# A shared opening for two output pairs, and a rearranged end of the convolution mixer, in a two-layer encoder

## The chip, the cores and the metric

The kernel runs on one core of a Trainium2 chip. The metric is device time in microseconds (us) of one execution, as the median of several runs. Line numbers (L12) are those of the kernel before the change.

## The reference, cut to what matters

An encoder of two layers over 256 positions and 2048 channels. Each layer is a mixer and a feed-forward part with a residual sum after each; the mixer of layer 0 is a convolution module, that of layer 1 a differential attention.

```
h = rmsnorm(x, mix_norm[0])
u = h @ w_in + b_in                       # 2048 -> 4096, halves a and gate
u = a * sigmoid(gate)
u = causal_dwconv(u, dw_w, dw_b)          # 31 taps per channel
u = silu(layernorm(u)) @ w_out + b_out    # layernorm over the 2048 channels
x = x + u
x = x + conv_ffn(rmsnorm(x))              # 2048 -> 2 * 5632 -> 2048
x = x + diff_attention(rmsnorm(x))        # 16 heads, relative bias, causal by chunks of 64
x = x + conv_ffn(rmsnorm(x)); out = rmsnorm(x)
```

## The kernel before, in words

Channels lie on the 128 partitions and positions along the rows; the 2048 channels are 16 tiles (`KT`), and x is held as eight double tiles `X[pr]`. A weight is loaded as 512 KB tiles of 128 x 1024 fp32 (`raw`, L140, on SP's DMA queue, five buffers). Each is split into a rounded part `hi` (a cast on ACT, L150) and a remainder `lo` (a subtraction, L152, on DVE or, where the step says "g", on POOL). Activations are split in the same way (L279 on ACT, L280 on DVE). A product is three: hi by hi, hi by the activation's remainder, lo by hi (L229).

The program is a list of steps, one weight tile each (`step`, L197); `pair` (L215) makes four steps of one pair of output tiles, 96 products in all. `run` (L178) goes through the steps: `ahead` (L186) asks for the tile four steps on to be split, then come the step's products, then what was put off to this step (`at`, L166), then `every` and the step's `post`. A scheduler places the instructions on the engines in the order of a modelled time; `high_priority`, `manual_schedule` and `issue_after` steer it.

**The opening.** `setup` (L391) loads x and the first weight tiles in turn on SP's queue, splits x (16 tiles) and the first weights, sums the squares of x on DVE (L333) and calls `norm_cols` (L336: sums over channels on PE, L286, then the power -1/2 on POOL, L298) and `norm_rows` (L351: spreads the result over the partitions with products L292, ACT copies it to `rstd`). The products of `w_in` don't need `rstd`; `post` (L449) does. It scales a pair by `rstd` (L453), takes the sigmoid (L455) and writes `cpad` (L457). There are two PSUM buffers `pp`, so the third pair needs the first one's `post`. The lo tiles of pair 0 are made on DVE, those of pair 1 on DVE and POOL in turn, and of pairs 2 to 15 on POOL.

**The taps.** For the 31-tap convolution `post` writes `cpad` to DRAM (`ud`, L469) and reads it back as four shifted copies `R` (L473), both on ACT's queue. `diagonals` (L481, POOL) makes small diagonal matrices `dg` (L482), and for pair 0 also the 18 full ones of the last tile (L489). `taps` (L493) does 12 taps of a tile (20 of tile 13, 24 of tile 14) on PE five steps later (L498); DVE does the rest, six per step (`tap_step`, L529). The last tile (i = 15) has 18 taps on PE (L507) and 13 on DVE (L515 to L519).

**The end of the mixer.** `dev` (L562) subtracts a shift from each tile, squares it, and sums both: on POOL up to tile 13 (L582, L583), in `early` for tile 14 (L591, L592, sums over channels L286), in `late` for tile 15. `layernorm` (L601) makes mean and variance, the power on POOL (L616), rows by products (L292) and then normalizes (L629 to L633) and activates (L637 to L645) tile by tile; the products of `w_out` (L238, L239), the first two pairs of it in alternation, start with the first tile.

**Attention's tables.** `attn_setup` (L746) runs in front of the first feed-forward step. On POOL's queue it writes a 3 MB table of shifted biases to DRAM in one DMA (L759), and then 16 small ones put the mask into it (L766). `bias` (L848) loads one head's 128 KB from it on SP's queue.

## Time and profile before

| | |
|---|---|
| median of 3 runs | 2254.43 us (2253.42 to 2255.34) |
| the profiled execution, its own time | 2254.46 us |
| its span, first to last instruction | 2252.7 us |
| PE busy | 2205.2 us (98% of the span) |
| DVE, ACT, POOL busy | 1634.2, 1200.7, 273.5 us |
| mean granted TensorE clock | 0.991 |

PE is TensorE's products, DVE is VectorE, ACT is ScalarE, POOL is GpSimd, SP is the engine whose queue issues most DMAs. A row of a timeline gives the start and the duration, the engine, the line, what is written and read, and in brackets how long the engine stood idle before it and what released it. The clock column is the granted share of TensorE's clock, 1.00 at 2.4 GHz and 0.50 at 1.2 GHz.

### The profile page before, as it was taken

How to read it: one execution, taken by the hardware profiler on the slowest of the kernel's cores; microseconds unless marked ns; L12 is line 12 of the kernel's file. 1: busy time of each engine (PE TensorE's matmuls, PEld its weight loads, DVE VectorE, ACT ScalarE, POOL GpSimd, SP SyncE). 2: the span in 40 equal slices, each digit the busy share in tenths (PEclk: the TensorE clock that was granted, in tenths of full speed). 3: DMA queues.
4: the chain of work that ended last, by engine and by line, in shares of the span. 5: the costliest groups of instructions: out<-in, count | busy, mean ns of one | idle time of the engine just before them, and what ended most of it. 6: DMA issues, size and time to landing. Idle time of an engine off the chain costs nothing.

```text
span 2252.7 us, 34458 instructions
## 1 busy us (share of the span) xinstructions
PE 2205.2 (98%) x13238; PEld 1937.4 (86%) x13238; DVE 1634.2 (73%) x2471; ACT 1200.7 (53%) x1796; POOL 273.5 (12%) x181
## 2 busy tenths in 40 slices
PE   5999899999999999999999999999999999999998
PEld 5999788888888888888888888888888888888887
DVE  4788675877767777677777787767777677676774
ACT  4333454655545555455565665555555455554554
POOL 4788500100000000000100000100000000000002
PEclk8999999999999999999999999999999999999998
DMA  6677357866666666666655555566666666666662
GB/s 236 192 218 215 112 185 164 244 187 189 188 189 191 189 188 187 192 189 186 193 176 177 171 171 174 170 192 186 190 187 187 188 188 187 190 188 190 187 188 94
DMA packets 126004, 417.51 MB, mean 185 GB/s; under 512 B 14416, under 2 KB 26704, under 8 KB 125840
## 3 DMA queue, kind: packets, MB, share of 16 engines
q1 hardware_dynamic: 113040, 400.42, 57.2%
q10 hardware_dynamic: 11520, 11.45, 2.0%
q0 software_dynamic: 1280, 3.46, 1.3%
q8 instruction: 103, 1.69, 0.3%
q14 instruction: 61, 0.50, 0.1%
HBM read 407.55 MB, written 7.72 MB: 184 GB/s over the span
## 4 chain that ended last, share of the span: by engine, by line
PE 94%; DMA 2%; DVE 0%; issue 0%; ACT 0%; POOL 0%; ACTq 0%; POOLq 0%; DVEq 0%
PE pp L238 48%; PE pp L239 25%; PE pp L229 7%; PE pp L236 4%; PE pp L235 2%; PE pp L813 1%; PE pp L815 1%; PE pp L814 1%; DMA raw<-in_w_up_dram 1%; PE s L863 1%; PE s L498 1%; PE o L898 0%; DMA R<-ud 0%; PE t L498 0%; PE s L507 0%; DMA ud<-cpad 0%
## 5 line engine op out<-in xcount | busy, mean ns | idle before, releaser
L238 PE MATMUL pp<-act,hi 128*128 128x512 f32 x3902 | 1380.7, 396 | 5.8 <-DVE act L645 3.1
L239 PE MATMUL pp<-act,lo 128*128 128x256 f32 x3902 | 1095.7, 281 | 0.0
L150 ACT CAST hi<-raw 128x1024 fp32r<-128x1024 f32 x752 | 788.1, 1049 | 532.2 <-PE pp L238 186.2
L152 DVE TENSOR_TENSOR lo<-raw,hi 128x1024 fp32r<-128x1024 f32 x686 | 844.4, 1232 | 299.2 <-ACT hi L150 287.5
L238 PEld LDWEIGHTS pp<-act,hi 128*128 128x128 f32 x3902 | 732.5, 188 | 165.6 <-DVE act L645 3.4
L239 PEld LDWEIGHTS pp<-act,lo 128*128 128x128 f32 x3902 | 739.4, 189 | 10.2
L238 PE MATMUL pp<-actb,hi 128*128 128x512 f32 x856 | 308.5, 397 | 1.4 <-ACT hi L150 1.4
L239 PE MATMUL pp<-actb,lo 128*128 128x256 f32 x856 | 241.3, 282 | 0.8 <-DVE lo L152 0.8
L333 POOL TENSOR_TENSOR ssq<-ssq,Z 128x512 f32<-128x512 f32 x24 | 35.6, 1484 | 1518.4 <-ACT Z L329 1518.3
L229 PE MATMUL pp<-act,hi 128*128 128x256 f32 x1088 | 203.4, 289 | 9.0 <-ACT act L279 6.2
L238 PEld LDWEIGHTS pp<-actb,hi 128*128 128x128 f32 x856 | 161.3, 188 | 40.2 <-ACT hi L150 1.7
L229 PEld LDWEIGHTS pp<-act,hi 128*128 128x128 f32 x1088 | 173.7, 196 | 15.5 <-ACT act L279 6.2
L152 POOL TENSOR_TENSOR lo<-raw,hi 128x1024 fp32r<-128x1024 f32 x66 | 158.0, 2413 | 56.3 <-ACT hi L150 55.6
L239 PEld LDWEIGHTS pp<-actb,lo 128*128 128x128 f32 x856 | 162.6, 190 | 1.2 <-DVE lo L152 1.1
L266 ACT COPY E<-pp 128x512 f32<-128x512 f32 x104 | 60.9, 585 | 184.1 <-PE pp L236 184.1
L229 PE MATMUL pp<-act,lo 128*128 128x256 f32 x544 | 156.4, 288 | 2.0 <-POOL lo L152 1.5
L382 ACT COPY E<-pp 128x512 f32<-128x512 f32 x109 | 63.9, 586 | 170.7 <-PE pp L236 163.0
L268 DVE TENSOR_TENSOR E<-pp,E 128x512 f32<-128x512 f32 x104 | 71.9, 691 | 108.2 <-ACT E L266 108.2
L704 DVE SCALAR_TENSOR_TENSOR Y<-fpad,prm,Y 128x256 f32<-128x256 f32 x352 | 146.9, 478 | 0.0
L384 DVE TENSOR_TENSOR x<-pp,x 128x512 f32<-128x512 f32 x101 | 69.8, 691 | 87.8 <-ACT E L382 87.4
L701 ACT ACTIVATE Y<-fpad,prm 128x256 f32<-128x256 f32 x176 | 96.3, 595 | 48.3 <-DVE fpad L697 48.3
L229 PEld LDWEIGHTS pp<-act,lo 128*128 128x128 f32 x544 | 106.7, 196 | 2.4 <-POOL lo L152 1.7
(194 smaller groups left out, 1797.5 us busy)
## 6 DMA issues: line engine op xcount, KB each, us to landing
raw<-in_w_up_dram SPq DMA_DIRECT2D x352, 512.0 KB, 4.1
raw<-in_w_down_dram SPq DMA_DIRECT2D x176, 512.0 KB, 4.1
raw<-in_w_in_dram SPq DMA_DIRECT2D x64, 512.0 KB, 4.4
raw<-in_w_qk_dram SPq DMA_DIRECT2D x64, 512.0 KB, 3.6
raw<-in_w_out_dram SPq DMA_DIRECT2D x32, 512.0 KB, 3.8
raw<-in_w_v_dram SPq DMA_DIRECT2D x32, 512.0 KB, 3.7
raw<-in_w_o_dram SPq DMA_DIRECT2D x32, 512.0 KB, 3.8
R<-ud ACTq DMA_DIRECT2D x52, 132.0 KB, 4.8
```

The lines of the kernel that those rows point to most:

```text
L150: nc.scalar.copy(hi[:, :n], raw[:, :n])
L152: ins = eng.tensor_tensor(lo[:, :n], raw[:, :n], hi[:, :n].bitcast(F32), ALU.subtract)
L229: nc.tensor.matmul(ps[:, 0:S], w[:, kk, cs], xt[:, x, :], start=(k == first and n == 0), stop=(k == last and n == 2))
L236: nc.tensor.matmul(*main, start=False, stop=True)
L238: nc.tensor.matmul(*main, start=(k == first), stop=False)
L239: nc.tensor.matmul(*corr, start=False, stop=False)
L266: nc.scalar.copy(cs, ps[:, :, S:])
L268: nc.vector.tensor_tensor(t, ps[:, :, 0:S], cs, ALU.add)
L382: nc.scalar.copy(cs, ps[:, :, S:])
L384: nc.vector.tensor_tensor(x, ps[:, :, 0:S], x, ALU.add)
L701: nc.scalar.activation(y[:, j, :], u[:, j, FK - 1:], AF.Identity, scale=self.col("fw", ch * FK + FK - 1), bias=self.col("fb", ch))
L704: nc.vector.scalar_tensor_tensor(y[:, j, :], u[:, j, q:q + S], self.col("fw", ch * FK + q), y[:, j, :], ALU.mult, ALU.add)
```

## The change

- **Opening.** Seven idle products on PE, while nothing is loaded. `X[0]` and `X[1]` go to ACT's queue; the weight tile 0 is loaded and split in two halves, and five weight tiles are loaded ahead instead of four. Pairs 0 and 1 are interleaved, so that every four tiles of x serve two weight tiles; pair 2 has its PSUM in the banks `s` and `t`. `norm_cols` runs after step 7 and `norm_rows` after step 8, `post` of pairs 0 and 1 two steps after their last product. The running sum of squares lies in PSUM.
- **POOL in the opening.** The lo tiles of pairs 0 to 2 are all made on DVE. Those of steps 12 to 16 are issued on POOL after the power. The full diagonals, 16 instead of 18, are made four at a time with pairs 1 to 4, after the lo tiles then at hand.
- **Tile 14.** Its `R` is copied straight from `cpad` in SBUF by 16 DMAs, eight on SP's queue and eight on ACT's. Its 24 taps on PE come three steps after `post`, inside pair 15, and its 7 on DVE one step after it (`few_taps`).
- **Tile 15.** `post` scales the two halves apart. 16 taps on PE and 15 on DVE, with the early sums after the thirteenth of PE's; the PSUM sum of PE is added last.
- **Sums.** The last additions in front of the early sums are made on POOL (they were on POOL and DVE). POOL's lo tiles after that point are issued after these sums, and after the layernorm's power.
- **Idle products** (`keep_warm`): five after the late sums, eight after the rows.
- **Attention's tables.** The table row goes to DRAM once, and 16 DMAs on SP's queue, one every eight steps, spread it; the mask is written by POOL into the loaded tile of a head. The zeroing of `kd` (L786) keeps its place in the program.

The diff, cut:

```diff
-        self.ND = 18
+        self.ND = 16
@@ load_w
+        n = w["n"] // 2 if i == 0 else w["n"]
+        for o in range(0, w["n"], n):
+            self.nc.sync.dma_start(w["raw"][:, o:o + n], w["src"][:, o:o + n])
@@ split_w
+            first = self.pow0 if 12 <= i < 17 else self.pool_first
+            with self.tc.issue_after(first) if w["lo_eng"] == "g" and first else ExitStack():
+                ins = eng.tensor_tensor(lo[:, p], raw[:, p], hi[:, p].bitcast(F32), ALU.subtract)
@@ x_square, norm_cols (first norm only)
+                st["ssq"] = self.psx("s", [P, 2, S])
+            self.nc.scalar.copy(f, q[:, 0, :])
+            self.nc.vector.tensor_tensor(f, q[:, 1, :], f, ALU.add)
@@ setup
+        warm = self.psx("t", [P, P])
+        for _ in range(7):
+            nc.tensor.matmul(warm, self.ones, self.ones, start=True, stop=True)
...
+            (nc.scalar if pr < 2 else nc.sync).dma_start(self.X[pr], a["x"][:, 2 * pr:2 * pr + 2, :])
...
-        self.norm_cols(n0)
-        self.norm_rows(n0)
+        self.todo[7] = [lambda: self.norm_cols(n0)]
+        self.todo[8] = [lambda: self.norm_rows(n0)]
@@ post
+                    for x in (1, 0):
+                        nc.vector.tensor_tensor(t[x], t[x], nin["rstd"], ALU.mult)
...
+                for j in range(4):
+                    for s in range(4):
+                        q = nc.sync if s < 2 else nc.scalar
+                        q.dma_start(R[s * 32:(s + 1) * 32, j, :n], u[j * 32:(j + 1) * 32, s:s + n])
...
-            queue = self.tc.issue_after(self.pool_lo) if i == 0 else ExitStack()
-            with queue:
+            with self.tc.issue_after(self.pool_lo) if i < 6 else ExitStack():
                 diagonals(i, g, dg)
-            self.at(5 if i < KT - 2 else 4, lambda: taps(i, u, R, dg))
+            if i == KT - 2:
+                self.at(1, lambda: few_taps(i, u))
+            self.at(5 if i < KT - 2 else 3, lambda: taps(i, u, R, dg))
@@ few_taps (new; DVE, on PSUM "o")
+            for n, j in enumerate(range(4 * c.G[i], CK)):
+                w = self.col("cw", i * CK + j)
...
+            st["few"] = self.b1("O")
+            nc.scalar.activation(st["few"], p, AF.Identity, bias=self.col("cb", i))
@@ last_taps
+                if j == 3 * len(dgl) // 4:
+                    st["early"] = self.const.tile([P, 4], F32, name="early")
+                    ps = sums(st["h"])
...
-            nc.scalar.copy(e, acc)
-            nc.vector.tensor_tensor(e, part[0], e, ALU.add)
-            dev(i, part[1], e)
+            nc.scalar.copy(e, part[0])
+            nc.vector.tensor_tensor(e, part[1], e, ALU.add)
+            dev(i, acc, e)
@@ dev
+                    for h, src in zip(st["h"], (d[:, i % 2, :], sq)):
+                        ins = nc.gpsimd.tensor_tensor(h, h, src, ALU.add)
+                self.pool_first = ins.ins
@@ layernorm
+            idle = self.pp.tile([P, 2, 512], F32, tag="pp", name=self.nm("pp"))
+            def keep_warm(n):
+                for _ in range(n):
+                    i = nc.tensor.matmul(idle[:, 0, :P], self.ones, self.ones, start=True, stop=True)
+                    self.tc.keep_in_program_order(i)
+            keep_warm(5)
...
-            nc.gpsimd.tensor_tensor(rc, v, self.mhalf, ALU.pow)
+            self.pool_first = nc.gpsimd.tensor_tensor(rc, v, self.mhalf, ALU.pow).ins
...
+            keep_warm(8)
@@ conv_module, the pairs of w_in
+                            (lambda ps, i=i: self.at(2, lambda: post(i, ps))) if i < 2 else lambda ps, i=i: post(i, ps),
+                            lo="v" if i < 3 else "g", merged=True,
+                            halves=(lambda: [self.psx(b, [P, 512]) for b in "st"]) if i == 2 else None)
+            if i == 1:
+                self.interleave(0)
@@ attn_setup, bias
+        nc.gpsimd.dma_start(tab, tb)
+            d = nc.sync.dma_start(d1[h], tab[h:h + 1, :].to_broadcast([P, 384]))
+            self.at(16 + 8 * h, lambda h=h: spread(h))
...
+            nc.gpsimd.memset(BM[h][:64, S - 64:], MASK)
```

## Rows read from the trace of the kernel before

**Rows 1.** Waits of PE over the whole span: us in total, times, longest.

```profile
PE o L292 <- POOL rc L298: 11.4, 2, 10.3
PE pp L229 <- ACT act L279: 6.2, 1, 6.2
```

**Rows 2.** Windows: length, busy time of PE, PEld, DVE, ACT, POOL, then clock.

```profile
6.18:20.00 13.82, 13.18 (x90) 12.89 (x91) 11.36 (x22) 11.07 (x21) 0.00 (x0) 1.00 1.02 389
36.00:49.43 13.43, 3.09 (x15) 2.79 (x15) 0.00 (x0) 1.04 (x1) 13.43 (x9) 0.63 0.48 150
52.87:62.00 9.13, 8.07 (x60) 7.72 (x64) 0.48 (x1) 1.22 (x3) 0.07 (x1) 0.82 0.71 192
62.00:226.90 164.90, 164.90 (x1508) 153.73 (x1501) 136.32 (x279) 60.56 (x71) 144.50 (x76) 1.00 0.72 208
```

**Rows 3.** Timeline of POOL in the opening.

```profile
30.81 5.04 POOL L489 TENSOR_TENSOR Y<-ident,cprm 128x512 f32<-128x512 f32 x4
...
37.18 11.55 POOL L152 TENSOR_TENSOR lo<-raw,hi 128x1024 fp32r<-128x1024 f32 x5
48.69 0.69 POOL L298 TENSOR_TENSOR rc<-c,mhalf 128x2 f32<-128x2 f32 x1
```

**Rows 4.** The chain that ended last: one pair, one tile's 12 taps, four row products.

```profile
86.67 11.71 PE pp L229 x96
98.38 1.43 PE s L498 x24
...
1118.51 0.44 PE o L292 x4
```

**Rows 5.** Groups of ACT and DVE, 0 to 36 us: busy, mean ns, idle before.

```profile
L150 ACT CAST hi<-raw 128x1024 fp32r<-128x1024 f32 x13 | 13.4, 1044 | 5.4 <-DMA raw<-in_w_in_dram 5.4
L279 ACT ACTIVATE act<-x,prm 128x256 fp32r<-128x256 f32 x16 | 7.0, 499 | 0.5 <-DMA x<-in_x_dram 0.5
L329 ACT ACTIVATE Z<-x 128x512 f32<-128x512 f32 x7 | 4.3, 626 | 2.4 <-DVE ssq L333 2.4
...
L152 DVE TENSOR_TENSOR lo<-raw,hi 128x1024 fp32r<-128x1024 f32 x6 | 8.7, 1446 | 8.4 <-ACT hi L150 8.4
```

**Rows 6.** Timeline of PE and DVE from the last pair to the first product of w_out.

```profile
241.39 2.80 PE L498 MATMUL t<-R,dg 128*32 128x256 f32 x48 [0.49 <-DMA R<-ud]
242.31 0.48 DVE L457 SCALAR_TENSOR_TENSOR cpad<-pp,prm,G 128x256 f32<-128x256 f32 x1 [0.68 <-ACT G L455]
244.11 7.18 PE L507 MATMUL s<-cpad,Y 128*128 128x256 f32 x32
251.99 0.95 PE L286 MATMUL o<-ones,M 128*128 128x2 f32 x8
253.72 1.36 DVE L786 MEMSET kd<- 64x256 f32 x4
255.51 0.58 PE L286 MATMUL o<-ones,act 128*128 128x2 f32 x4 [2.57 <-DVE act L569]
258.06 2.08 PE L292 MATMUL s<-ident,c 128*128 128x128 f32 x8 [1.53 <-POOL c L616]
263.23 0.80 PE L238 MATMUL pp<-act,hi 128*128 128x512 f32 x1 [3.10 <-DVE act L645]
```

**Rows 7.** Windows: the late sums, the first products of w_out; columns as in rows 2.

```profile
253.00:257.00 4.00, 1.03 (x8) 0.97 (x8) 2.20 (x9) 0.57 (x2) 0.89 (x2) 1.00 0.03 5
...
264.00:268.00 4.00, 4.00 (x15) 3.42 (x14) 3.89 (x9) 3.35 (x8) 3.85 (x4) 0.53 0.00 0
```

**Rows 8.** A window of the first feed-forward part, columns as in rows 2.

```profile
378.00:412.00 34.00, 30.27 (x163) 25.77 (x162) 14.71 (x23) 13.11 (x21) 6.19 (x12) 0.95 0.98 199
```

**Rows 9.** DMA issues: size of one, median us from issue to landing.

```profile
d<-Z POOLq DMA_DIRECT2D x1, 3072.0 KB, 36.4
```

**Rows 10.** A head's bias tile in attention, from issue to landing.

```profile
DMA to landing us min/median/max: 2.5/3.5/4.1
```

More of the change, by code (lines that the diff above doesn't have):

```diff
@@ L332, in x_square @@
             else:
-                (eng or nc.gpsimd).tensor_tensor(st["ssq"], st["ssq"], sq, ALU.add)
+                (nc.vector if st["first"] else nc.gpsimd).tensor_tensor(st["ssq"], st["ssq"], sq, ALU.add)
         st["n"] += 1
@@ L339, in norm_cols @@
         f = self.b1("M")
-        self.nc.vector.tensor_tensor(f, q[:, 0, :], q[:, 1, :], ALU.add)
+        if st["first"]:
+            self.nc.scalar.copy(f, q[:, 0, :])
+            self.nc.vector.tensor_tensor(f, q[:, 1, :], f, ALU.add)
+        else:
+            self.nc.vector.tensor_tensor(f, q[:, 0, :], q[:, 1, :], ALU.add)
         srcs = [f]
@@ L414, in setup @@
         with self.tc.manual_schedule(engines={ET.DVE, ET.Activation, ET.Pool}):
-            for pr in range(KT // 2):
-                if pr % 2 == 0 and pr // 2 < 4:
-                    self.split_w()
-                for j in range(2):
-                    m = 2 * pr + j
-                    n0["xh"][m] = self.act_tile()
-                    self.split_act(n0["xh"][m][1], self.X[pr][:, j, :], self.col("mixg", m))
-            for pr in range(KT // 2):
-                if pr % 3 == 2:
-                    self.ahead(4 + pr // 3)
-                self.x_square(n0, pr, nc.vector)
-        self.norm_cols(n0)
-        self.norm_rows(n0)
+            for m in range(KT):
+                if m in (0, 2):
+                    first = self.split_w() if m == 0 else first
+                    next(first)
+                elif m % 4 == 0 and m < 12:
+                    self.ahead(self.ns)
+                n0["xh"][m] = self.act_tile()
+                self.split_act(n0["xh"][m][1], self.X[m // 2][:, m % 2, :], self.col("mixg", m))
+                if m % 4 == 3 and m < 12:
+                    self.ahead(self.ns)
+                if m % 4 == 3 and m > 4:
+                    for pr in (m // 2 - 3, m // 2 - 2):
+                        self.x_square(n0, pr)
+            for pr in (KT // 2 - 2, KT // 2 - 1):
+                self.x_square(n0, pr)
+        self.todo[7] = [lambda: self.norm_cols(n0)]
+        self.todo[8] = [lambda: self.norm_rows(n0)]
         self.fpad = []
@@ L434, in setup @@
         self.cpad = []
-        for i in range(3):
+        for i in range(4):
             t = self.ph1.tile([P, S + CK + 1], F32, name=f"cpad{i}", bufs=1)
@@ L586, in dev, with sums @@
             nc.scalar.activation(sq, d[:, i % 2, :], AF.Square)
-            ps = self.psx("o", [P, 8])
-            if i == KT - 2:
-                h = [self.b1("M"), self.b1("M")]
-                for x, (src, add) in enumerate(((st["sd"][1], d[:, 0, :]), (st["sq"], sq))):
-                    nc.gpsimd.tensor_tensor(h[x], src[:, 0, :], src[:, 1, :], ALU.add)
-                    nc.vector.tensor_tensor(h[x], h[x], add, ALU.add)
-                    self.chan_sums(ps[:, 4 * x:4 * x + 4], [h[x]])
-                st["early"] = self.const.tile([P, 4], F32, name="early")
-                nc.scalar.mul(st["early"], ps.rearrange("p (a b) -> p a b", b=2)[:, :, 0], 1.0 / c.D)
-            else:
-                for x, src in enumerate((d[:, 1, :], sq)):
-                    self.chan_sums(ps[:, 4 * x:4 * x + 4], [src])
-                st["late"] = ps
+            if i == KT - 2:
+                with self.tc.high_priority():
+                    for h, src in zip(st["h"], (d[:, i % 2, :], sq)):
+                        ins = nc.gpsimd.tensor_tensor(h, h, src, ALU.add)
+                self.pool_first = ins.ins
+            else:
+                st["late"] = sums((d[:, i % 2, :], sq))
+        def sums(srcs):
+            ps = self.psx("o", [P, 8])
+            for x, src in enumerate(srcs):
+                self.chan_sums(ps[:, 4 * x:4 * x + 4], [src])
+            return ps
         def layernorm():
@@ L965, in encoder @@
     KT = cfg.KT
-    n0 = b.new_norm("mixg", 0)
+    n0 = b.new_norm("mixg", 0, first=True)
     n1 = b.new_norm("ffng", 0)
```

122 lines of the change are left out of this document (73 added, 49 removed).

## The prediction

> **What bounds it now.** First the waits of PE over the whole span: PE is 98% busy by the table, so only its gaps and its time at half clock can be won. The longest wait is 10.3 us for the power L298, in the opening; next come 6.2 us before the first product [rows 1]. The windows say where the rest lies: between 36 and 49.43 PE works 3.09 us at a clock of 0.63, and from 52.87 to 62 it still has gaps at 0.82; from 62 to 226.9 it has no gap at a clock of 1.00, so in that stretch nothing is to be won [rows 2]. The timeline of POOL names the cause of the 10.3 us: the sums were ready by about 36, but five lo tiles (11.55 us, from 37.18) stand ahead of the power at 48.69, and 5.04 us of diagonals ahead of those [rows 3]. Two smaller places are left: the chain from the last pair to the first product of w_out [rows 6, 7], and the start of the first feed-forward part, where the 3 MB table is written [rows 8, 9].
>
> **The opening: the sum.** A pair is 11.71 us, a weight tile a quarter of it, 2.93; a tile's 12 taps are 1.43 [rows 4]. Before, pair 2 begins at 52.87 [rows 2]. After, three limits compete for the first eight tiles (pairs 0 and 1):
> - PE alone: 6.18 + 8 x 2.93 = 29.6. One group of four x tiles now feeds 5.9 us of products instead of 2.9, so data come at half the rate per product.
> - ACT: 8 casts of 1.04, 16 splits of 0.44 and 8 squares of about 0.6 are 8.3 + 7.0 + 4.9 = 20.2 us [rows 5]. The first product at 6.18 stood 1.5 us (a cast and a split) after ACT began, so ACT is through at 4.7 + 20.2 + about 1 for loads = 26; then lo of the last tile, 1.2 to 1.4 [rows 5], and its products 2.9: 30.3.
> - Tile 6, cast behind the squares, is split at about 25 and then two tiles of products follow: 26 + 5.9 = 32.
>
> I take 32, and 0.5 for the channel sums (0.95 for twice as many [rows 6]): step 8 begins at **32.5**. It doesn't wait for the power: pair 2 has banks of its own, and sums, power (0.69 [rows 3]) and hops fit under step 8, if POOL is empty. It is: the first 12 lo tiles are DVE's and tile 12 is held back. From 32.5: 13 pairs (152.2), 13 groups of taps (18.6), rows 0.44 [rows 4], and 0.4 for the shift's products give 204.1 for the end of pair 14. The same sum from 52.87, with the gap (1.06) and the half clock (0.18 x 9.13 = 1.6) of 52.87 to 62, gives 226.7 against 226.9. I add 1.3 for stalls that I can't see: 205.4, **a gain of 21.5**. Bounds: 25.3 (PE alone, no stall) and 14 (second rival).
>
> Costed at nothing, with what hides it:
> - Six more lo tiles on DVE (7.4 us): DVE is idle from 36 to 49.43 [rows 2]; if PE's products come as early as forecast, DVE is asked for them before 32, where it had 8.4 us of waits for casts [rows 5].
> - The power's new successors: tile 12 is needed at step 12, some 12 us after the power; POOL makes one per 2.31 (11.55 / 5 [rows 3]).
> - Full diagonals, 1.26 each [rows 3], four of them in pairs 1 to 4: POOL is busy 144.5 of 164.9 [rows 2], so 20 us are free for 5.
> - Three posts close together (steps 8, 9, 11) queue their DMAs on ACT, and R of pair 2 waits for the taps of pair 0; the casts behind it have four steps of lead (11.7 us).
> - X[0], X[1] on ACT's queue, tile 0 in halves, five loads ahead: the transfers were at 389 GB/s up to 20 us [rows 2], so the order moves the first product by about 1 either way; ACT's 20.2 us hide it.
> - Idle products at the start: 14 instructions at 0.26 (2.08 / 8 [rows 6]) are 3.6 us, over before 6.18. Ninety products took 13.82 us where full clock needs 11.0 [rows 2, 4], so at most 2.8 us lie there; ACT limits by then, so I count none.
>
> **The end of the mixer.** From the end of pair 14 (226.9) to the first product of w_out (263.23) it is 36.3 us [rows 2, 6]. After: pair 15 11.7, taps of tiles 13 (2.4, 20 of 24 parts of 2.80) and 14 (2.8, now inside the pair): 16.9. PE then waits for the last post, with nothing to put there: u was complete 1.9 after the pair's end (240.9 to 242.8); in halves some 1.6. Sixteen taps are 16/18 of 8.0 (244.11 to 251.99 [rows 6]) = 7.1, and the early sums 0.95 lie between them. Then the last addition and PE's sums of it, 0.5 and 1.0 and a hop; before, 2.57 us passed there, with 1.36 of kd's zeroing ahead of L569 on DVE [rows 6]. Up to here 16.9 + 1.6 + 8.05 + 1.7 = 28.3; then mean, variance and power 1.55 (PE's wait was 1.53), rows, and 3.1 to the first product [rows 6]. Rows at full clock are 0.9 for 2.08 (0.44 for four [rows 4]). Sum 28.3 + 1.55 + 0.9 + 3.1 = 33.9, a gain of 2.4. At the head of w_out the clock was 0.53 for 4 us [rows 7], 1.9 us of work, but ACT hands out tiles at 0.84 each (3.35 for four [rows 7]), so nearly nothing of it counts. The lo tiles held back behind POOL's power have 8 us and more until steps 68 to 71. The 16 DMAs of R pass SP's weight loads: eight issues are about 3 us, three steps are 8.8 and the taps of tile 13 another 2.4. I take **2.2**, between -1 and 4.5.
>
> What that rests on is the clock. In 253 to 257 PE was busy 1.03 of 4 us and still had 1.00; then it ran the rows at 0.26 each, the half level [rows 6, 7]. The ten and sixteen idle instructions lie in the waits of 1.53 and 3.1 if each takes 0.11, and overrun by 1.1 each if it takes 0.26: that is the -1. The Trainium skill, "TensorE: Matmul & The Clock Gate", section "Why this matters for your kernels", says that idle gaps between bursts of products throw the engine back to half rate; by that rule the filled gaps keep the rate and the sum has the 2.4. No run here yet shows idle products.
>
> **The first feed-forward part.** In 378 to 412 PE is idle 3.7 us, and the mean clock of 0.95 costs 34 x 0.05 = 1.7 more [rows 8]; the 16 DMA engines were full (0.98), and the 3 MB DMA took 36.4 [rows 9]. Spread into 16 pieces it should cost PE nothing: **5.0**, between 3 and 5.4. In attention POOL's writing of the mask waits for the head's tile, 3.5 us after issue [rows 10], and the head's power waits behind it on POOL, then DVE's scaling. PE waited for a power only twice [rows 1], so for no head's, and tiles are split four steps ahead: nothing.
>
> **Sum.** 21.5 + 2.2 + 5.0 = 28.7. The profiled execution took 2254.46, as the median (2254.43): 2225.8, say **2226**.
>
> **Rivals.**
> 1. *The sums come late.* They stand on DVE and ACT behind the lo tiles and casts of tiles 6 to 11. If all six added lo tiles (7.4) come first, step 8 begins at 40 and the opening gives 14: 2233. For it: strict queues; against: the buffers of lo hold six, so tiles 10 and 11 can't come early. Chance 0.18.
> 2. *The power isn't freed.* If the holding back fails or another POOL job (diagonals, 5.04) is placed ahead, the wait of 10.3 stays in good part; of the opening 11 are left: 2236 to 2241. For it: the scheduler orders POOL by modelled time; against: only tiles 12 to 16 are near and are tied to the power. Chance 0.07.
> 3. *Slower: the spread of the table.* It sits on SP's queue, with the weight loads, for some 136 steps. The 3 MB took 36.4 us in one piece; a piece is 2.3 us. If each stopped PE for its whole length, 36.4 would come on top: 2262. It decides from 1.8 us a piece (28.7 / 16) on. Against: the undivided write, with the DMA engines full for 34 us, cost PE 5.4 in all [rows 8]. Chance 0.04.
>
> **How the numbers follow.** The forecast has 0.71. Its bounds are 25.3 + 4.5 + 5.4 = 35.2 (2219) and 16 + 0 + 3 = 19 (2235). With most of rival 1 and a part of rival 2 the range is 2217 to 2239. A measurement can tell 0.2%, 4.5 us, from no change: faster in the forecast and rivals 1 and 2 (0.96 together, of which I give 0.02 to a gain eaten up elsewhere), slower in rival 3.
>
> **What would show it.** Right: PE's wait for L298 of 10.3 gone, pair 2 beginning near 32, the end of pair 14 near 205, the first product of w_out some 34 later at 1.00, no gap of PE in the 34 us where the table was written. Wrong: PE waiting at L286 for the sums (rival 1), POOL with lo tiles ahead of the power (2), PE waiting for casts on raw in the first feed-forward part (3); new gaps of PE between 33 and 90, for taps or POOL's lo, would say that the cover which I named isn't there.

## The result, and the profile after

The changed kernel takes **2229.39 us** (median of 4 runs, 2228.45 to 2230.25) against 2254.89 before in the same comparison (4 runs, 2253.42 to 2257.07): a ratio of 0.9886, 95% interval 0.9869 to 0.9903. The prediction had 2226, with 2217 to 2239. The profiled execution took 2228.45 us, its span is 2226.7 (2252.7 before), the mean clock 0.997 (0.991). Line numbers below are those of the kernel that a row belongs to; in the changed one L240 are w_in's products, L542 the taps on R, L566 the last tile's, L164 lo, L309 the opening's power, L488 and L485 the scaling by `rstd`, L493 the writing of `cpad`.

The waits of PE over the whole span:

```profile
PE s L542 <- DMA R<-ud: 2.7, 2, 1.8
PE o L297 <- DVE act L632: 2.5, 1, 2.5
PE pp L240 <- ACT act L290: 1.9, 2, 1.7
...
PE pp L240 <- DVE cpad L493: 1.2, 1, 1.2
PE s L566 <- DVE cpad L493: 1.1, 1, 1.1
```

The wait of 10.3 for the power [rows 1] is gone. The 6.2 for the first tile are only filled with the idle products: the first product of w_in starts at 6.12 instead of 6.18. What stands first now are waits for R of the first pairs (2.7), and those at the end of the mixer (2.5, 1.1 and 1.1). Windows of the changed kernel, columns as in rows 2 (the last two, behind the clock, are the busy share of the DMA engines and GB/s):

```profile
32.30:44.00 11.70, 11.70 (x100) 11.70 (x100) 2.87 (x6) 5.05 (x7) 4.61 (x4) 1.00 0.43 141
45.85:62.00 16.15, 13.48 (x124) 12.35 (x125) 3.27 (x7) 4.25 (x5) 16.15 (x9) 1.00 0.94 229
62.00:208.70 146.70, 146.70 (x1349) 136.22 (x1349) 123.87 (x273) 54.54 (x65) 132.12 (x73) 1.00 0.78 221
...
237.00:241.00 4.00, 3.59 (x22) 3.29 (x22) 2.14 (x4) 0.21 (x1) 2.40 (x2) 0.68 0.00 0
246.00:250.00 4.00, 4.00 (x21) 3.29 (x22) 3.85 (x8) 2.97 (x8) 3.92 (x4) 1.00 0.18 68
378.00:412.00 34.00, 34.00 (x197) 29.80 (x196) 25.92 (x40) 19.67 (x28) 0.00 (x0) 1.00 0.65 197
```

Pair 2 starts at about 32.3 and runs without a gap: 36 to 49.43 was the hole of before [rows 2]. From 45.85 to 62 PE misses 2.67 us; from 62 to the end of pair 14 nothing. The statistics (237 to 241) run at 0.68, but w_out starts at 1.00 where it had 0.53 [rows 7]. From 378 to 412 us, where the table's writing fell before, PE is busy throughout; before, 3.7 us and 5% of the clock were missing there [rows 8]. POOL in the opening, to be laid beside rows 3:

```profile
39.39 0.70 POOL L309 TENSOR_TENSOR rc<-c,mhalf 128x2 f32<-128x2 f32 x1 [38.95 <-DVE c L308]
40.04 2.41 POOL L164 TENSOR_TENSOR lo<-raw,hi 128x1024 fp32r<-128x1024 f32 x1
```

Nothing stands ahead of the power any more. It comes at 39.39 because its sums do, not because of POOL. The first mark of the table below is DVE's scaling behind the last product of pair 14, in the kernel before and in the changed one:

```profile
226.94 0.70 DVE L453 TENSOR_TENSOR pp<-pp,rstd 128x512 f32<-128x512 f32 x1 [0.96 <-PE pp L229]
208.66 0.70 DVE L488 TENSOR_TENSOR pp<-pp,rstd 128x512 f32<-128x512 f32 x1 [0.96 <-PE pp L240]
```

**Where the 26.0 us of span came from**, by marks of the two traces:

| | before | after | gain | forecast |
|---|---|---|---|---|
| end of pair 14 | 226.94 | 208.66 | 18.3 | 21.5 |
| from there to the first product of w_out | 36.3 | 37.3 | -1.1 | 2.2 |
| from there to the table's product in the first feed-forward part | 103.5 | 101.9 | 1.5 | 0 |
| from there to the first product with V in attention | 737.1 | 730.9 | 6.2 | 5.0 |
| the rest | | | 1.1 | 0 |

Two rows are not shown to be gains of the change. The third stretch took 101.4 us in the first run below, whose kernel is that of before from the end of the opening on. The rest lies behind the last pair: the sums of the last norm took 1.29 us instead of 1.61, and from its power to the next work on POOL it was 1.74 instead of 2.58, but 2.58 again in the run with pairs 0 and 1 in turn, which leaves that part as the change has it.

### The profile page after: what moved, and what is told of

Read it like the earlier page. It is cut to its first block, busy times and chain, and to the rows that moved or that the text cites. A ratio compares the mean times of both kernels' runs of the same rounds, so it can differ in the third digit from the quotient of the medians.

```text
span 2226.7 us, 34566 instructions
## 1 busy us (share of the span) xinstructions
PE 2202.7 (99%) x13274; PEld 1935.3 (87%) x13274; DVE 1629.1 (73%) x2482; ACT 1200.9 (54%) x1799; POOL 251.1 (11%) x175
## 4 chain that ended last, share of the span: by engine, by line
PE 95%; issue 2%; DVE 1%; POOL 1%; DMA 1%; ACT 0%; POOLq 0%; ACTq 0%
PE pp L249 49%; PE pp L250 25%; PE pp L240 6%; PE pp L247 4%; PE pp L246 2%; PE pp L900 1%; PE pp L902 1%; PE pp L901 1%; PE s L952 1%; PE s L542 1%; DMA R<-ud 1%; PE o L987 0%; POOL lo L164 0%; PE s L249 0%; DVE s L599 0%
## 5 line engine op out<-in xcount | busy, mean ns | idle before, releaser
L164 DVE TENSOR_TENSOR lo<-raw,hi 128x1024 fp32r<-128x1024 f32 (+1 forms) x693 | 849.8, 1228 | 286.7 <-ACT hi L160 285.2
L160 ACT CAST hi<-raw 128x1024 fp32r<-128x1024 f32 (+1 forms) x753 | 788.0, 1047 | 499.8 <-PE pp L249 190.9
L249 PEld LDWEIGHTS pp<-act,hi 128*128 128x128 f32 x3902 | 731.6, 187 | 161.5 <-ACT hi L160 1.4
L250 PEld LDWEIGHTS pp<-act,lo 128*128 128x128 f32 x3902 | 737.1, 189 | 9.8
L347 POOL TENSOR_TENSOR ssq<-ssq,Z 128x512 f32<-128x512 f32 x24 | 35.9, 1496 | 1549.1 <-ACT Z L343 1549.0
L240 PE MATMUL pp<-act,hi 128*128 128x256 f32 x1024 | 188.5, 286 | 3.1 <-ACT act L290 1.9
L240 PEld LDWEIGHTS pp<-act,hi 128*128 128x128 f32 x1024 | 160.7, 193 | 9.4 <-issue 4.9
L240 PE MATMUL pp<-act,lo 128*128 128x256 f32 x512 | 145.4, 284 | 0.3 <-DVE lo L164 0.3
L164 POOL TENSOR_TENSOR lo<-raw,hi 128x1024 fp32r<-128x1024 f32 x60 | 142.8, 2406 | 14.3 <-ACT hi L160 7.3
L599 DVE SCALAR_TENSOR_TENSOR s<-cpad,cprm,s 128x256 f32<-128x256 f32 x182 | 85.2, 486 | 20.2 <-PE s L542 16.8
```

Source lines behind the costliest of these rows:

```text
L160: nc.scalar.copy(hi[:, p], raw[:, p])
L164: ins = eng.tensor_tensor(lo[:, p], raw[:, p], hi[:, p].bitcast(F32), ALU.subtract)
L240: nc.tensor.matmul(ps[:, 0:S], w[:, kk, cs], xt[:, x, :], start=(k == first and n == 0), stop=(k == last and n == 2))
L249: nc.tensor.matmul(*main, start=(k == first), stop=False)
L250: nc.tensor.matmul(*corr, start=False, stop=False)
L599: nc.vector.scalar_tensor_tensor(acc, u[:, j:j + S], self.col("cw", i * CK + j), acc, ALU.mult, ALU.add)
```

## The experiments

All are in this order of subject: the opening, the end of the mixer, the table, and versions put together. "Pair 14" is the start of the scaling that ends it (208.66 in the changed kernel). The marks come from one trace of each version, and they scatter: five versions with the changed kernel's opening have pair 14 at 208.54 to 209.92, three with the pairs in turn at 206.78 to 207.42.

### The POOL queue alone

The kernel before, with the added lo tiles moved to DVE, those of steps 12 to 16 held back behind the power, and the diagonals of pair 0 no longer tied to a place behind a lo tile of POOL's.

```diff
-                            lo="v" if i == 0 else "vg" if i == 1 else "g", merged=True)
+                            lo="v" if i < 3 else "g", merged=True)
+        with self.tc.issue_after(self.pow0) if 12 <= i < 17 else ExitStack():
...
-            queue = self.tc.issue_after(self.pool_lo) if i == 0 else ExitStack()
+            queue = ExitStack()
```

> The kernel before with one part of the change: the lo tiles of pairs 0 to 2 on DVE, those of steps 12 to 16 behind the power on POOL; nothing interleaved, no idle products. Theory (POOL's queue was the loss): PE's wait of 10.3 us for the power falls below 2 us, pair 2 begins near 40 instead of 52.87, pair 14 ends near 214 instead of 226.9, total near 2241. Rival (the opening was short of data, and the shared opening is what helps): pair 2 begins after 47, total 2249 or more.

2244.12 us (2241.15 to 2244.88), ratio 0.9957 (0.9941 to 0.9974). POOL's timeline:

```profile
37.99 0.70 POOL L299 TENSOR_TENSOR rc<-c,mhalf 128x2 f32<-128x2 f32 x1 [12.44 <-DVE c L298]
38.64 4.67 POOL L153 TENSOR_TENSOR lo<-raw,hi 128x1024 fp32r<-128x1024 f32 x2
```

The power comes at 37.99 instead of 48.69 [rows 3], PE's wait for it falls from 10.3 to 1.0, pair 2 begins at 41.76 instead of 52.87, and pair 14 ends at 216.64, **10.3 earlier**. That this is the length of the old wait is partly chance: PE now waits 3.4 us for lo tiles on DVE (0.5 before), and 3.1 of other waits went (2.0 for the sums fell to 0.4, 1.5 for a lo tile on POOL to nothing). That the queue of POOL was the cause is shown; so is that it is little more than half of the opening's 18.3. The theory's marks (pair 2 near 40, pair 14 near 214, total near 2241) were missed by 2 to 3 us.

### Pairs 0 and 1 in turn, and pair 2's own banks

First the changed kernel without the interleaving: pair 0, then pair 1, with before's order of splits and the posts at the step where the sums are ready.

```diff
-            (lambda ps, i=i: self.at(2, lambda: post(i, ps))) if i < 2
+            (lambda ps, i=i: self.at(5 - 3 * i, lambda: post(i, ps))) if i < 2
...
-            if i == 1:
-                self.interleave(0)
```

> The changed kernel with pairs 0 and 1 one after the other again, and x and the tiles split in the order of before; everything else of the change stays. Theory (POOL's queue): pair 14 ends 1 to 4 us later than the 208.6 of the changed kernel, total 2230 to 2233. Rival (data): 8 us later or more, total 2237 or more.

2228.72 us (2228.27 to 2230.23), ratio 0.9889 (0.9874 to 0.9904): the same as the changed kernel. Pair 14 ends at 207.39, 1.3 *earlier*. Pair 2 begins 1.7 later (33.92 against 32.24), since PE stands idle 1.0 us between 20 and 30 and has 71 products there instead of 86. But the sums stand behind 192 products instead of 246, so the power comes at 34.34, and PE waits neither for `cpad` nor for R: behind the start of pair 2 it waits 1.4, for a lo tile, instead of 3.8, and the sums (0.5) are done by then. So the shared opening wins 1.7 ahead of pair 2 and loses 2.9 behind it; taken whole it wins nothing, and what the change gained there came with it, not from it.

Then this version without pair 2's banks `s` and `t`, the norm right behind step 7 (pair 0's post comes a step sooner, and the first diagonals wait for the power):

```diff
-    halves=(lambda: [self.psx(b, [P, 512]) for b in "st"]) if i == 2 else None)
+    halves=None)
-        self.todo[8] = [lambda: self.norm_rows(n0)]
+        self.todo[7].append(lambda: self.norm_rows(n0))
```

> The run with pairs 0 and 1 in turn, and pair 2 in the buffers pp like all others: it waits again for sums, power, rows and the post of pair 0, which come right behind the last product of pair 1. Theory (with POOL freed, what is left of the opening's gain is that pair 2's products cover the statistics): PE waits about 5.5 us there (sums 1, power 1.5, rows 0.9, scaling, sigmoid and cpad 2.2) and some of it at half clock after, so that pair 14 ends 5 to 8 us later than the 207.4 of the run in turn; total 2234 to 2237. Rival (idle products and the first loads make that part): pair 14 ends within 2 us of 207.4.

2233.27 us (2231.54 to 2234.56), ratio 0.9912 (0.9897 to 0.9927); PE now waits for the norm's chain again:

```profile
PE pp L240 <- DVE cpad L488: 2.2, 1, 2.2
PE o L303 <- POOL rc L309: 1.0, 1, 1.0
```

Pair 14 ends at 212.11, so the banks, with the cover that they give the statistics, are worth **4.7**, a little less than the 5 to 8 expected. The runs make a ladder for the end of pair 14: 226.94 before, 216.64 with POOL's queue freed, 212.11 with the other edits of the opening (idle products, the first loads, the sums behind step 7 and in PSUM, the diagonals spread over the pairs, a fourth `cpad`), 207.39 with pair 2's banks, 208.66 with the pairs interleaved. The step of 4.5 in the middle holds several edits that were not tried one by one.

### The idle products at the start

```diff
-        for _ in range(7):
-            nc.tensor.matmul(warm, self.ones, self.ones, start=True, stop=True)
```

> The changed kernel without the seven idle products at the start. Theory (the first tiles wait for x and for casts, so the level of the clock doesn't count): the first tiles run at half clock, and pair 14 still ends within 0.7 us of 208.6. Rival (PE is the limit of the opening, so half clock is paid): pair 14 ends 1.5 to 3 us later.

2230.41 us (2230.06 to 2231.71), ratio 0.9899 (0.9883 to 0.9916). From 6 to 20 us this version has 95 products where the changed kernel has 91, and 86 in each from 20 to 30: the idle products give the first ones nothing. In the changed kernel the 14 idle instructions end at 4.41, PE then stands idle for 1.71 us, and from 7 to 9 us both versions have 11 products where they have 19 from 13 to 15. (The clock column reads 1.00 in both windows; the pace of the products, 0.63 us for two against 0.40 later, was the half one in the first.) Pair 2 begins 0.5 earlier here, at 31.76. Pair 14 still ends 2.1 later, at 210.80, the size that the rival gave, but not for its reason; the reason is in PE's waits between 20 and 215:

```profile
PE s L539 <- DMA R<-ud: 5.2, 3, 1.9
PE pp L240 <- DVE cpad L490: 1.2, 1, 1.2
```

It waits 5.2 for R instead of 2.7, the same kind of stall that the changed kernel has. Why R is later here, although the sums come 0.5 earlier, no run shows.

### The sums earlier

If those stalls come from posts that are late and close together, squaring x earlier must shrink them.

```diff
-                if m % 4 == 3 and m > 4:
-                    for pr in (m // 2 - 3, m // 2 - 2):
+                if m % 4 == 3 and 4 < m < 12:
+                    for pr in range(4) if m == 7 else (4, 5):
```

> The changed kernel with the squares of x moved up: four double tiles of x are squared ahead of the casts of weight tiles 8 to 11, two ahead of the last ones, so that the channel sums stand behind 234 products instead of 246. Theory (the posts of pairs 0 to 2 come late and bunch, and PE's waits of 1.16 for cpad and 0.82 and 1.85 for R follow from that): sums 1.2 us earlier or more, the waits shrink by as much each, pair 14 ends at 206 to 207.2 instead of 208.66, total 2227 to 2228.5. Rival (the three posts are bunched whatever the sums do, and the transfers of R are limited by the DMA engines, whose share is over 1.0 there): the same waits, pair 14 within 0.6 of 208.66. Against both: casts that come later behind the squares may cost PE waits for weight tiles 10 and 11, 1 us or so.

2227.21 us (2225.64 to 2228.23), ratio 0.9881 (0.9867 to 0.9896). The power is at 38.21 instead of 39.39, and of PE's waits between 20 and 215 this is left:

```profile
PE s L542 <- DVE s L599: 1.0, 1, 1.0
PE s L542 <- DMA R<-ud: 0.5, 1, 0.5
```

Waits of 3.8 shrink to 1.5, pair 14 ends at 206.36, **2.3 earlier** and 1.0 earlier than with the pairs in turn. The theory's range was met at its early end: with the sums 1.2 us earlier, 2.3 of stalls went. That the one follows from the other in this measure rests on one trace; in the run without idle products the sums were 0.5 earlier and the waits for R grew.

### R of pairs 0 and 1 straight from SBUF

The change copies tile 14's R from `cpad` by 16 DMAs. Would the same help the pairs whose R is late?

```diff
-            if i < KT - 2:
+            if 1 < i < KT - 2:
                 ud = self.dr.tile([P, UW], F32, tag="ud", name=self.nm("ud"), bufs=2)
```

> The changed kernel with the R of pairs 0 and 1 copied from cpad in SBUF by 16 DMAs each (as the change does for tile 14) instead of through DRAM. Theory (two hops one after the other, write and read back, make R of the first pairs late): PE's two waits for R, 2.7 us in all, go, pair 14 ends at 206 to 207 instead of 208.66. Rival (DMA engines are full there, share 1.02 to 1.15, or the 16 issues on two queues delay weight loads and casts): waits stay or move to the weight tiles or to R of pair 2, pair 14 within 1 of 208.66 or later.

2241.0 us (2239.32 to 2244.0), ratio 0.9945 (0.993 to 0.9959): **11.6 slower** than the changed kernel (pair 14 ends at 220.37), the rival's way (issues that delay weight loads and casts), at a size that it did not give. SP's queue (DMA issues, from first to last):

```profile
30.81 14.86 SPq L143 DMA_DIRECT2D raw<-in_w_in_dram  x5
45.73 11.96 SPq L516 DMA_DIRECT2D R<-cpad  x16
57.78 16.14 SPq L143 DMA_DIRECT2D raw<-in_w_in_dram  x6
```

and one wait of ACT between 36 and 100, and the longest of PE between 36 and 215:

```profile
ACT hi L160 <- DMA R<-cpad: 7.2, 1, 7.2
...
PE t L542 <- POOL lo L164: 3.8, 1, 3.8
PE t L542 <- DMA R<-ud: 3.0, 1, 3.0
PE s L542 <- DMA R<-cpad: 2.5, 1, 2.5
```

For 12 us no weight load is issued on SP, and a cast stands 7.2 us behind the copies that ACT has to issue. The copies themselves are late too. For tile 14 in the changed kernel the same eight issues take 5.42 us on SP and 5.15 on ACT, at a place where the weights are ahead; in the opening they are not. The price of such copies is the issuing queue, not the bytes: 16 of 33 KB are 528 KB a tile, where the way through DRAM moves 144 and four times 132, 672.

### The end of the mixer

The changed kernel from pair 15's end to w_out, PE's and then DVE's rows and two of POOL's (start, duration, and in brackets the idle time before):

```profile
222.55 2.80 PE L542 MATMUL t<-R,dg 128*32 128x256 f32 x48
226.45 5.85 PE L566 MATMUL s<-cpad,Y 128*128 128x256 f32 x26 [1.10 <-DVE cpad L493]
...
236.91 0.58 PE L297 MATMUL o<-ones,act 128*128 128x2 f32 x4 [2.53 <-DVE act L632]
...
237.79 1.89 PE L682 MATMUL pp<-ones 128*128 128x128 f32 x10
239.48 1.11 PE L303 MATMUL s<-ident,c 128*128 128x128 f32 x4
241.68 1.22 PE L303 MATMUL s<-ident,c 128*128 128x128 f32 x4 [1.10 <-DVE c L695]
242.70 3.18 PE L682 MATMUL pp<-ones 128*128 128x128 f32 x16
246.00 0.50 PE L249 MATMUL pp<-act,hi 128*128 128x512 f32 x1
...
225.48 0.42 DVE L632 TENSOR_TENSOR act<-t,O 128x256 f32<-128x256 f32 x1 [1.93 <-PE t L542]
225.82 0.48 DVE L493 SCALAR_TENSOR_TENSOR cpad<-pp,prm,G 128x256 f32<-128x256 f32 x1
...
234.67 1.36 DVE L873 MEMSET kd<- 64x256 f32 x4 [0.27 <-DMA raw<-in_w_out_dram]
...
239.34 2.29 DVE L695 TENSOR_TENSOR c<-mom,c 128x2 f32<-128x2 f32 x1 [0.82 <-POOL c L694]
...
238.60 0.70 POOL L694 TENSOR_TENSOR c<-c,mhalf 128x2 f32<-128x2 f32 x1 [6.12 <-DVE c L693]
239.27 4.65 POOL L164 TENSOR_TENSOR lo<-raw,hi 128x1024 fp32r<-128x1024 f32 x2
```

Four things lie on the path. Tile 14's taps run behind pair 15, not inside it, and on DVE the last `cpad` (L493) stands behind tile 14's difference (L632), which waits for those taps: PE then waits 1.10 for `cpad`. The zeroing of `kd` still costs 1.36. The product of mean and power, two columns, takes 2.29 us: POOL's held-back lo tile starts 0.07 before it. And the clock falls in spite of the idle products: it reads 1.00 up to 238 and 0.50 from 239 to 245. Each was tried.

How much one of them is worth is hard to read from the whole stretch, which scatters by itself. From pair 14 to w_out, the seven versions that leave the changed kernel's end as it is took 36.0 to 39.7 us (37.3 in the changed kernel), the two with the end of before 36.3 and 37.1. So what follows goes by single rows first.

**The idle products round the statistics left out.**

```diff
-            keep_warm(5)
-            keep_warm(8)
```

> The changed kernel without the thirteen idle products round the statistics. Theory (they don't hold the clock, which fell before the rows in the changed kernel too, but raise it for the first products of w_out): the first product of w_out within 0.5 us of 246.0, the stretch from there to the tables' product 1 to 2 us longer than 101.9. Rival (they stand in the way): the first product of w_out more than 0.6 us earlier, and the tables' product no later than 347.9.

2231.3 us (2229.38 to 2232.54), ratio 0.9903 (0.9888 to 0.9918). The window 238 to 250, in this version:

```profile
238.00:250.00 12.00, 6.38 (x23) 5.32 (x24) 7.23 (x15) 3.66 (x9) 9.48 (x7) 0.50 0.28 88
```

The same window in the changed kernel:

```profile
238.00:250.00 12.00, 10.79 (x55) 9.60 (x55) 8.64 (x18) 5.04 (x13) 10.93 (x8) 0.72 0.28 88
```

The idle products raise the clock's mean from 0.50 to 0.72, but from the end of PE's late sums to the first product of w_out it is 8.07 us without them and 8.06 with them, and from there to the table's product 101.9 in both. They bought nothing that can be measured; neither theory nor rival had that. The first product of w_out is 1.4 later here because another DVE operation met one of POOL's (the tap described below, 1.42 us instead of 0.66), and the sums ran at half the clock. Behind it the half clock lasts to 251, but PE waits for nothing there up to the table's product, where the changed kernel waits 1.4 us: what the clock costs, the waits give back.

**The product of mean and power on POOL**, behind the power and ahead of the lo tiles.

```diff
-            nc.vector.tensor_tensor(mr, mean, rc, ALU.mult)
+            self.pool_first = nc.gpsimd.tensor_tensor(mr, mean, rc, ALU.mult).ins
```

> The changed kernel with the product of mean and power made on POOL, behind the power, instead of on DVE; the lo tiles follow it. Theory (DVE's 2.29 us for two columns is a wait for POOL's lo tile beside it): the second rows no longer wait, and the stretch from the end of pair 14 to the first product of w_out falls from 37.4 to about 36. Rival (the idle products or ACT set the start): it stays within 0.4 of 37.4.

2228.71 us (2228.16 to 2229.33), ratio 0.9888 (0.9873 to 0.9903). Rows of POOL and DVE of this version:

```profile
226.25 1.27 POOL L647 TENSOR_TENSOR lnsq<-lnsq,Z 128x512 f32<-128x512 f32 x1
...
240.20 0.20 POOL L695 TENSOR_TENSOR c<-mom,c 128x2 f32<-128x2 f32 x1
...
226.21 1.59 DVE L578 SCALAR_TENSOR_TENSOR pp<-cpad,cprm,mp 128x256 f32<-128x256 f32 x1
```

The product takes 0.20, and from the start of the late sums to w_out it is 7.71 us instead of 9.09. The whole stretch is 36.9, between theory and rival: 0.9 was lost ahead of the sums, as the first of DVE's last taps, which reads `cpad` and `mp` from SBUF, took 1.59 instead of 0.66 beside POOL's addition. The thirteen taps with one operand in PSUM are not touched (6.79 in both).

**The zeroing of `kd` on POOL as well.**

```diff
-                self.tc.keep_in_program_order(nc.vector.memset(t[d, cc, :].bitcast(F32), 0.0))
+                self.tc.keep_in_program_order(nc.gpsimd.memset(t[d, cc, :].bitcast(F32), 0.0))
```

> The run with the product of mean and power on POOL, and the zeroing of kd moved from DVE to POOL besides. Theory (the 1.36 us of zeroing lie on the path from DVE's last tap to the last addition): the stretch from the end of pair 14 to the first product of w_out falls by 1.0 to 1.4 us from the 36.9 of that run. Rival (PE's last taps and the early sums set that point): it stays within 0.4.

2227.97 us (2227.06 to 2227.98), ratio 0.9888 (0.9873 to 0.9903). From pair 14 to w_out it is 34.2 instead of 37.3. That is the length that the prediction had (36.3 less 2.2), but by luck: tile 14's taps and the wait of 1.10 still stand behind pair 15. Against the run before it is 2.7 less, more than the 1.0 to 1.4 expected, because besides the zeroing DVE's first tap took 0.55 this time. PE's wait before the late sums is 1.60 instead of 3.46, and behind it the clock held:

```profile
238.00:250.00 12.00, 10.33 (x69) 8.95 (x69) 8.37 (x21) 6.90 (x16) 10.82 (x9) 1.00 0.28 88
```

The span gained only 0.5 on the changed kernel. 1.0 was given back behind w_out's first product (102.9 instead of 101.9), about half of it in waits of PE. And pair 14 ended 1.3 later. The waits for R and `cpad` are the same there (3.8), but the first products ran longer at the half level:

```profile
6.00:20.00 14.00, 13.11 (x80) 12.38 (x81) 10.92 (x19) 10.60 (x20) 0.00 (x0) 0.76 1.04 391
```

These are 80 products against 91, with the same idle products ahead of them.

### The table as before

```diff
-            self.at(16 + 8 * h, lambda h=h: spread(h))
-            nc.gpsimd.memset(BM[h][:64, S - 64:], MASK)
```

(and before's writing of the 3 MB in one DMA and of the masks in its place)

> The changed kernel with attention's tables written as before (one 3 MB DMA and 16 mask DMAs on POOL's queue). Theory (the undivided write starves the weight loads): the stretch from the tables' first product to the end of the first feed-forward part grows by 5 to 6.5 us, from 725.3 to about 731, with idle PE and half clock again where the DMA engines are full; total near 2235. Rival (that stretch is shorter for another reason, the order of the first loads): it grows by less than 2 us, total 2231 or less.

2238.58 us (2236.38 to 2239.29), ratio 0.993 (0.9915 to 0.9945). A stretch of 96 us with the table's writing in it, in this version:

```profile
344.00:440.00 96.00, 91.64 (x510) 78.58 (x510) 65.52 (x97) 51.52 (x73) 10.05 (x18) 0.98 0.81 205
```

The stretch of the same work in the changed kernel:

```profile
340.00:436.00 96.00, 96.00 (x550) 83.28 (x549) 71.50 (x105) 56.19 (x81) 1.21 (x2) 1.00 0.62 190
```

From the table's product to V's first product it is 737.8 us here, 730.9 in the changed kernel, 737.1 before: the spreading is worth **6.2 to 6.9**. The window says where: 4.4 us without products, and 2% of the clock on 91.6 us, 1.8. The total is above the expected 2235, as another 3.9 us were lost ahead of the table, in the end of the mixer (39.7 instead of 37.3) and behind w_out's first product (103.6 instead of 101.9), where the two kernels do the same work.

### Put together

Pairs 0 and 1 in turn (its edits are shown above) with both edits on POOL:

```diff
-            if i == 1:
-                self.interleave(0)
...
+            self.pool_first = nc.gpsimd.tensor_tensor(mr, mean, rc, ALU.mult).ins
+                self.tc.keep_in_program_order(nc.gpsimd.memset(t[d, cc, :].bitcast(F32), 0.0))
```

> The version with pairs 0 and 1 in turn and, at the end of the mixer, the mean times the power and the zeroing of kd on POOL. Theory (the gains are independent): pair 14 ends at 207.4, the first product of w_out 34.2 later at 241.6, total 2226 less 0 to 1: 2225 to 2226.5, some 3 under the changed kernel. Rival (what is won in front of w_out is given back behind it, where ACT hands out the tiles, 1.0 in the run with both edits on POOL): 2226.5 to 2228.

2226.94 us (2225.86 to 2227.44), ratio 0.9882 (0.9865 to 0.9898), span 2224.1. Pair 14 ends at 206.78, the first product of w_out is at 242.80: 36.0, not 34.2. DVE's first tap met POOL again (1.42 instead of 0.55), and the ten idle instructions before the rows ran 2.48 us where they take 1.36 at full clock, so that the rows came 0.5 after what they need was there. The theory's sum for this stretch was missed by the part that depends on who meets whom; the total lies in the rival's range.

And with tile 14's difference behind the last `cpad` on DVE:

```diff
-                self.at(1, lambda: dev(i, acc, st["few"]))
+                st["acc14"] = acc
...
+            dev(i - 1, st["acc14"], st["few"])
+            acc = self.psx("s", [P, S])
...
+                with self.tc.issue_after(st["post15"]):
+                    nc.vector.tensor_tensor(d[:, i % 2, :], acc, rest, ALU.add)
```

> The same with the difference of tile 14, which waits for PE's taps of tile 14, issued on DVE behind the writing of the last cpad. Theory (in the changed kernel the last cpad stood behind that difference, and PE waited 1.1 us for it although it had the 2.8 us of tile 14's taps to work on): PE goes from tile 14's taps to the 16 of tile 15 with a wait under 0.2, the first product of w_out comes about 1 us sooner than without the edit, total 0.5 to 1.1 less. Rival (DVE's fifteen taps, not PE's sixteen, end the chain, or the sums of tile 14 on POOL come later and the early sums hold PE): the wait of 1.1 goes and comes back before the early or the late sums, total within 0.4.

**2225.93 us** (2224.75 to 2226.35), ratio 0.9875 (0.9861 to 0.989), span 2222.9. PE's rows:

```profile
221.31 2.80 PE L538 MATMUL t<-R,dg 128*32 128x256 f32 x48
224.03 5.88 PE L563 MATMUL s<-cpad,Y 128*128 128x256 f32 x26
...
242.08 0.50 PE L249 MATMUL pp<-act,hi 128*128 128x512 f32 x1 [1.30 <-DVE act L722]
```

The wait of 1.10 is gone and did not come back: from pair 14 (207.42) to w_out it is 34.7, 1.4 less than without the edit. This version has the lowest median, though its times overlap with those of the run before. Its first product of w_out is 3.9 us ahead of the changed kernel's and its span 3.8 shorter. The two were measured in different comparisons, and the intervals of their ratios overlap; but the lists of their times do not (2226.35 at most against 2228.45 at least, with medians of before 1.5 apart, 2253.37 and 2254.89). The earlier sums (206.36 for pair 14) were not tried on top of it.

## Why the prediction was right, and where it was wrong

**What bounds the kernel: right.** The opening and the table, two of the three places named, gave 24.5 of the 26.0, and POOL's queue ahead of the power was the largest single cause (10.3 of 18.3, shown by the first run). The second rival had priced that queue at the same: "of the opening 11 are left" of 21.5. That the total came within 3 us of the forecast is partly luck: the opening and the end of the mixer fell short by 3.2 and 3.3, while 1.2 more at the table and 2.6 in stretches whose gain is not shown to come from the change made up for much of it.

**The opening, 21.5 forecast, 18.3 measured.** The start of pair 2 came out as worked out (32.3 against 32.5), and the terms behind it hold: 171.6 for pairs, taps and rows. What failed is *"sums, power (0.69 [rows 3]) and hops fit under step 8, if POOL is empty"* and with it the 1.3 for stalls. The rows of the changed kernel:

```profile
35.01 0.88 DVE L364 TENSOR_TENSOR M<-M,Z 128x256 f32<-128x256 f32 x2
38.61 0.51 PE L297 MATMUL o<-ones,M 128*128 128x2 f32 x4
45.85 0.50 PE L240 MATMUL pp<-act,hi 128*128 128x256 f32 x2 [1.16 <-DVE cpad L493]
```

M for the sums was ready at 35.9 (35.01 + 0.88 on DVE), but the scheduler put PE's sums at 38.61, behind two tiles of pair 2. Power, rows and scaling then end 1.2 after pair 2, and three posts in a row make R late: 1.2 + 0.8 + 1.9 = 3.8 of stalls. With the sums' 0.5, which were counted ahead of step 8, that is 171.6 + 3.8 + 0.5 = 175.9 of the 176.4 from 32.3 to 208.66. It is the first rival in another form: the sums were late, yet PE waited not for them but for what follows them. The line *"Three posts close together (steps 8, 9, 11) queue their DMAs on ACT, and R of pair 2 waits for the taps of pair 0"* was costed at nothing for the casts, rightly (one stood 5.6 us behind R's issues on ACT, and PE waited for none), and at nothing for R, wrongly. The run with the earlier sums bears it out: 2.3 of the 3.8 went.

Of the rest of the 21.5 the prediction did not say which edit earns it. It let the shared opening carry it; the pairs in turn do as well, 1.7 later at pair 2 and with 2.9 less behind its start. In its bounds the 14 belongs to the first rival, not the second, and the lower bound of the whole was added up with 16 and 0 where the terms have 14 and -1; nothing hangs on it, since the measured gain lies well inside.

**The idle products at the start**, counted at nothing, gave the first tiles nothing (95 against 91 products by 20 us without them). The reason given, that ACT limits by then, is doubtful. The first products ran at half pace with them as without, and where that lasted longer, in the run with `kd` zeroed on POOL, pair 14 came 1.3 later.

**The end of the mixer, 2.2 forecast, -1.1 measured, just outside the lower bound of -1.** Up to the late sums the sum had 28.3, measured 29.3 (208.66 to 237.94). Up to the last tile's taps on PE it came out a little better than forecast (17.8 against 18.5): tile 14's taps went behind pair 15 instead of inside it, and of the 1.6 counted for the last post a wait of 1.10 is left, the price of one DVE operation in the wrong place of its queue; the last run takes that off. What failed is the step *"before, 2.57 us passed there, with 1.36 of kd's zeroing ahead of L569 on DVE"*: it took the zeroing as gone, but the change leaves it where it was, and from the last of those taps to the end of the late sums 3.6 passed where 1.7 was counted. Behind them it had 5.55, measured 8.06; the time up to the rows (1.5) and behind them (3.1) is as forecast, and the whole difference lies in the rows, 3.4 us instead of 0.9. 1.1 of that is PE's wait for DVE's product of mean and power, and the failed step is *"The lo tiles held back behind POOL's power have 8 us and more until steps 68 to 71"*: true of their users, but not of DVE's product beside them, which took 2.29 (0.16 in the kernel before). The other 1.4 is the clock: the idle products were forecast to hold it, and the rows ran at the half level, 1.11 and 1.22 instead of 0.44 each. The "overrun by 1.1 each" is not what cost: the eight after the rows took 3.18 us, but w_out's first tile was not ready sooner, and without them the time is the same. By the Trainium skill, "TensorE: Matmul & The Clock Gate", section "Why this matters for your kernels", idle gaps of PE between bursts are what loses the clock; the runs agree in direction (238 to 250 had 1.00 with a gap of 1.60 before the late sums, 0.72 with one of 2.53). Idle products behind the gap did not repair that in time for the rows. Since the same end took 36.0 to 39.7 us in seven versions, the sign of the -1.1 is not certain, but that the 2.2 were not won is.

**w_out's head**: *"nearly nothing of it counts"* was right about the clock: in the run without idle products, with 0.50 up to 251, the stretch to the table's product is the same 101.9. That it is 1.5 shorter than before is not shown to come from the change: across the versions it lies between 101.4 and 103.6, with the waits of PE that fall into it.

**The table, 5.0 forecast between 3 and 5.4, measured 6.2 to 6.9**: right in mechanism, mis-sized. The sum took 3.7 of idle time and 1.7 of clock, and then 5.0 for their 5.4. But the 34 us of rows 8 hold 163 products, where the changed kernel has 197 in as many: 34 products, at 34 / 197 = 0.17 us each, are 5.9. PE's waits in the whole stretch before are the same 3.8, which leaves 2.2 for the half clock where 1.7 was counted. The third rival did not occur: no piece of the spread table stops PE.

## What to carry to other kernels

A power on two columns can cost ten microseconds if long work of no hurry stands ahead of it on its queue: hold that work back behind the power. But look what else the held-back work then meets: at the end of the mixer it met a two-column product on DVE, which took 2.29 us where before it took 0.16. When a wait is removed, follow the chain one step on: statistics that no longer stop PE can still make the next transfers late, and in one run it paid to bring them 1.2 us forward (2.3 us less of stalls). And before a gain of one or two microseconds is put down to an edit, look how far the same stretch moves between versions that leave it alone.

## What the runs showed of the hardware that was not expected

- A DVE operation with both operands in SBUF waited for a whole operation of POOL, or held POOL up: 2.29 us for two columns beside a lo tile of 2.33, and 1.42 and 1.59 for a tap that takes 0.55 alone, beside a POOL addition of 1.27. Where the tap began 0.3 us ahead of that addition (226.34 and 226.66 in the changed kernel), the tap took 0.66 and the addition 1.46. Taps with an operand in PSUM keep their 0.52 (6.79 / 13). The Trainium skill, "SBUF — State Buffer", section "SBUF: two separate sides", tells of a pair of ports that the two share under an exclusive lock held for the instruction; the rows agree.
- Eight copies of a sixteenth of R each, from SBUF to SBUF, occupied the issuing queue for 5.15 and 5.42 us, 0.64 to 0.68 each, and nothing was seen to start behind them on SP or ACT meanwhile; the prediction had estimated 3.
- The 26 idle instructions round the statistics raised the granted clock there (0.50 to 0.72), and changed the time from the late sums to w_out by 0.01 us (8.06 against 8.07). In the first version put together, the ten before the rows held them up by 0.5.
